# One-hot tiles of the gate matrix, laid out token by token and made by one compare-and-scale instruction per token

## The chip, the cores and the metric

The kernel runs on one core of a Trainium2 chip. The metric is device microseconds (us) of one execution, lower is better. A NeuronCore has a matrix engine (TensorE, PE in the profile; its weight loads stand apart as PEld), a vector engine (DVE), a scalar engine (ACT), GpSimd (POOL) and a queue engine that only issues transfers (SP). Each engine runs its own instruction stream in order; semaphores order the streams against each other. The operands lie in SBUF, matmul results in PSUM. [...]

## The reference, cut to what matters

Two layers, each a token mixer followed by a PEER feed-forward block with 128 x 128 = 16384 experts. The block picks 128 experts for each of 512 tokens by product keys (8 heads, 16 each) and weighs them with a softmax:

```
s, i = lax.top_k(scores, PEER_TOPK)
cand_s = s[..., 0, :, None] + s[..., 1, None, :]
top_s, sel = lax.top_k(cand_s, PEER_TOPK)
gate = jax.nn.softmax(top_s, axis=-1)
act = gelu(einsum('td,ted->te', hx, u_sel))
out = einsum('te,ted->td', gx * act, v_sel)
```

The first 128 tokens are computed by gathering rows of `peer_u` and `peer_v`. For the other 384 tokens the kernel works densely over all experts: it needs a matrix G of gates, G[i, j, token], zero but for the 128 chosen experts (i, j) of a token. That matrix is the sum over the 128 chosen of onehot(j) x onehot(i) x gate, which is a matmul of two one-hot matrices per token, contracted over the chosen experts.

## The kernel before

A layer is a mixer (L324 on) and `peer` (L826 on). In `peer` come the query projections with the first top-16 search, then a routing part in which several kinds of work are blended, then a dense part (L1122 on) that goes over 128 chunks of 128 experts.

The routing part works through a list `main` of steps with weights (WC, WP, WG, WT, WO, meant as relative lengths): `cands`, eight `pick`s and `gates` per group of 128 tokens, `spread_sel`, and for each of the 48 blocks of eight tokens a step `onehot` of weight WO. `blend` sprinkles two other lists over `main` in proportion to the weights: 68 chunks of the dense hidden layer computed ahead (`s_ahead`, L857: 24 matmuls of 384 columns each, with operands split into a high and a low part) and the gathers of the first tokens. The list is cut in three parts; the third holds all the one-hot steps. With the weights of before the parts get 10, 10 and 48 of the 68 chunks. A scheduler then sets the order of each engine's stream.

One chunk takes weights through `split_next` (L255): ACT makes the high part, and DVE or POOL, in turns, the low part (L266, tile `wsp`). `gather_load` (L867) is issued on POOL, `gather_use` (L873) runs on DVE. `pick` (L971 to L983) runs top-16 searches and compares on DVE and a product on POOL (L983). `gates` has two integer instructions with an immediate scalar on DVE (L998, L999).

A one-hot step (L1026 to L1040) handles eight tokens with tiles of 128 partitions (the chosen experts) by 128 x 8 halfwords, the eight tokens innermost. Four instructions of 1024 elements make the four tiles: `oi` (L1035, DVE: equal to the index i), `x2` (L1036, POOL: times the low part of the gate), `x1` (L1037, DVE: times the high part) and `oj` (L1038, DVE). One row `sel[n]` of eight tokens is broadcast over the 128 columns. Then `onehot_mm` (L1042) runs the block before: for each token two matmuls (L1055), `oj` as the stationary and `x1`, then `x2` as the moving operand, so 16 matmuls of 128 columns per block and 768 per layer. Neighbouring columns of one token lie eight halfwords apart. ACT moves the results out (L1057). Three sets of tiles rotate; L1037, L1038 and L1036 of a block wait for the matmuls of an earlier block in the same set.

Of the kernel before, what the change touches and what calls it, by code (L numbers as in the profile page):

```python
# [11 lines left out]
F16 = mybir.dt.float16  # L12
# [3 lines left out]
ALU = mybir.AluOpType  # L16
# [3 lines left out]
P = 128  # L20
# [8 lines left out]
NK = 128  # L29
# [12 lines left out]
APER, AOFF, ADEL = 2, 1, 4  # L42
SIDE = (0, 1, 2, 3, 13, 18, 8, 9, 10, 11, 14, 15, 16, 17)
TAILW = 0.0
WC, WP, WG, WT, WO = 3.0, 2.8, 3.0, 1.0, 1.9
GSP = 0.9
GEND = 4
PO = 1
# [11 lines left out]
TB = 8  # L60
# [49 lines left out]
def body(ctx, tc, A, tap=None):  # L110
    nc = tc.nc
    V, S, G, TE = nc.vector, nc.scalar, nc.gpsimd, nc.tensor
# [11 lines left out]
    def nm(p):  # L124
        cnt[0] += 1
        return f"{p}{cnt[0]}"
# [3 lines left out]
    def bank(shape=(P, T)):  # L130
        return psp[0].tile(list(shape), F32, tag="ps", name=nm("ps"))
# [4 lines left out]
    def s2t(name, shape=(P, T), dt=F32):  # L136
        return s2.tile(list(shape), dt, tag="s2", name=nm(name))
# [12 lines left out]
    def C(n):  # L150
        o, w = COFF[n]
        return const[:, o:o + w]
# [673 lines left out]
    def peer(l):  # L826
        with ExitStack() as pctx:
# [6 lines left out]
            sel = {n: m.tile([P, TD], F16, name=f"sel{n}") for n in ("i", "j", "g1", "g2")}  # L834
# [27 lines left out]
            pace, adas = {}, []  # L862
# [38 lines left out]
            with ExitStack() as rctx:  # L901
                rt = rctx.enter_context(tc.tile_pool(name=f"route{l}", bufs=1))
                rpool[:] = rt, 3
                SV = [s2t("SV", (P, NH, 2, TOPK)) for _ in range(NT)]
                SF = [s2t("SF", (P, NH, 2, TOPK)) for _ in range(NT)]
                iot = rt.tile([P, NK, TB], F16, name="iot")
                G.tensor_copy(iot, C("iota").unsqueeze(2).to_broadcast([P, NK, TB]))
                keys = []
                for q in range(4):
                    kq = s2t("keys", (P, 4, P))  # L910
# [113 lines left out]
                gbs, ohr, pend = {}, [], []  # L1024

                def onehot(b):  # L1026
                    if not ohr:
                        ohr.extend([[s2t("oh", (P, NK, TB), F16) for _ in range(4)] for _ in range(3)])
                    oj, oi, x1, x2 = ohr[b % 3]
                    t0 = b * TB  # L1030

                    def bc(n):
                        return sel[n][:, t0:t0 + TB].unsqueeze(1).to_broadcast([P, NK, TB])

                    V.tensor_tensor(oi, iot, bc("i"), op=ALU.is_equal)  # L1035
                    pace["G"] = G.tensor_tensor(x2, oi, bc("g2"), op=ALU.mult)  # L1036
                    V.tensor_tensor(x1, oi, bc("g1"), op=ALU.mult)  # L1037
                    pace["V"] = V.tensor_tensor(oj, iot, bc("j"), op=ALU.is_equal)  # L1038
                    onehot_mm()
                    pend.append(b)  # L1040

                def onehot_mm():  # L1042
                    if not pend:
                        return
                    b = pend.pop()
                    oj, oi, x1, x2 = ohr[b % 3]
                    t0 = b * TB
                    if t0 % GB == 0:
                        gbs[0] = rt.tile([P, NK, GB], F32, tag="gb", name=nm("gb"), bufs=2)
                    gb = gbs[0]  # L1050
                    for t4 in range(TB // 4):
                        pt = bank((P, 4, NK))
                        for tt in range(4):
                            for q, xg in enumerate((x1, x2)):
                                TE.matmul(pt[:, tt], oj[:, :, t4 * 4 + tt], xg[:, :, t4 * 4 + tt], start=(q == 0), stop=(q == 1))  # L1055
                        o = t0 % GB + t4 * 4
                        S.activation(gb[:, :, o:o + 4].rearrange("p i t -> p t i"), pt, AF.Copy, scale=1.0 / GSC)  # L1057
                    if t0 % GB == GB - TB:
                        nc.sync.dma_start(gd[t0 // GB], gb)
# [23 lines left out]
                for t in range(1, NT):  # L1083
                    oh = [(WO, lambda b=b: onehot(b)) for b in range((t - 1) * P // TB, t * P // TB)]
                    nx = steps(t + 1) if t + 1 < NT else []
                    for i in range(len(oh)):
                        main.append(oh[i])
                        if nx:
                            main.append(nx.pop(0))
                    main += nx  # L1090
# [6 lines left out]

                main.insert(-EG, (0.0, early_ge))
                main += [(0.5, onehot_mm), (TAILW, lambda: None)]
                sl = [lambda c=c: s_ahead(c) for c in range(SPILL)]  # L1100
                gs = [lambda n=n: gather_step(n) for n in range(GPRE + 2)] if GPRE else []
                cuts = [0, len(steps0), len(steps0 + steps1), len(main)]
                ws = [sum(w for w, _ in main[a:b]) for a, b in zip(cuts, cuts[1:])]
                at = [0, round(SPILL * ws[0] / sum(ws)), round(SPILL * (ws[0] + ws[1]) / sum(ws)), SPILL]
                g1 = int(GFRAC * len(gs))
# [5 lines left out]
                for i, g in enumerate(gf):  # L1111
                    n = w - (i == NG // w - 1)
# [155 lines left out]
    for l in range(L):  # L1268
        mixer(l)
        peer(l)  # L1270
# [56 lines left out]
```

## Time and profile before

| | before |
|---|---|
| median of 3 runs, us | 3853.39 (3843.79 to 3864.01) |
| profiled execution: span, us | 3864.3 |
| PE busy, us (share) | 3636.7 (94%) |
| DVE busy, us (share) | 3061.0 (79%) |
| POOL busy, us (share) | 2206.7 (57%) |
| ACT busy, us (share) | 1494.1 (39%) |
| L1055, one-hot matmuls | 1536, busy 374.7 us |
| L1036, product on POOL | 96, busy 208.4 us |
| L1035, L1037, L1038 on DVE | 96 each, busy 96.9, 106.4 and 192.9 us |

The profile gives no time of the profiled execution other than its span, which is 0.3 us above the slowest of the three timed runs and 10.9 us above their median; what lies around the span is too small to be seen here. Matmuls are pipelined: one starts before the last has ended, so the busy time of PE counts each instant once, and the distance from start to start says what one matmul costs in a stream. The same holds on DVE, where an instruction starts a little before the one ahead of it has ended.

### The profile page before, as it was taken

What the parts mean: (1) busy time and instruction counts of PE and PEld (TensorE: products, weight loads), DVE (VectorE), ACT (ScalarE), POOL (GpSimd) and SP (SyncE); (2) the same over time, 40 slices, a digit from 0 to 9 for tenths busy, and PEclk for the clock granted to TensorE, in tenths of its full rate; (3) what the DMA queues carried; (4) which work ended last, traced back from release to release, by engine and by line L of the source; (5) the groups of instructions that cost most, each with busy time, mean ns of one, the idle gap of its engine ahead of it and who ended that gap; (6) DMA issues with size and microseconds to landing.
All of it is one profiled execution on the core that took longest, in us unless ns stands there. A gap on an engine that the chain in (4) does not pass through costs nothing. (4 is left out here: it accounts for less than half of the span.)

```text
span 3864.3 us, 51554 instructions
## 1 busy us (share of the span) xinstructions
PE 3636.7 (94%) x18154; PEld 3097.8 (80%) x18154; DVE 3061.0 (79%) x5457; ACT 1494.1 (39%) x2361; POOL 2206.7 (57%) x1440
## 2 busy tenths in 40 slices
PE   5999898899999999999998999999999999999998
PEld 4787688778788888888776877887888888888887
DVE  4765489988659999999848456999886798778888
ACT  4443263344443333333353424334344433333333
POOL 3532285656446677887627204366554566767765
PEclk7886799889789999999988789998887999999999
DMA  5223253455469999999713224245554899889885
GB/s 180 77 67 103 93 186 119 159 181 179 154 227 336 340 338 322 330 331 330 265 60 93 66 77 143 90 141 177 179 170 174 308 340 336 286 303 315 308 297 214
DMA packets 349859, 810.70 MB, mean 210 GB/s; under 512 B 45216, under 2 KB 178080, under 8 KB 346272
## 3 DMA queue, kind: packets, MB, share of 16 engines
q1 hardware_dynamic: 275872, 538.94, 41.5%
q0 software_dynamic: 73728, 268.47, 19.3%
q8 instruction: 142, 2.33, 0.2%
q14 instruction: 117, 0.96, 0.1%
HBM read 722.89 MB, written 84.41 MB: 209 GB/s over the span
## 5 line engine op out<-in xcount | busy, mean ns | idle before, releaser
L283 PE MATMUL pss<-hi,wsp 128*128 128x384 f32 (+1 forms) x5168 | 1148.0, 378 | 47.5 <-DVE wsp L266 15.7
L1174 PE MATMUL ps<-vv,wg 128*128 128x512 f32 x4608 | 1098.8, 396 | 58.9 <-ACT wg L1147 29.7
L283 PEld LDWEIGHTS pss<-hi,wsp 128*128 128x128 f32 x5168 | 1021.1, 208 | 120.4 <-DVE wsp L266 17.9
L1174 PEld LDWEIGHTS ps<-vv,wg 128*128 128x128 f32 x4608 | 867.7, 190 | 257.3 <-ACT wg L1147 38.5
L266 POOL TENSOR_TENSOR wsp<-raw,wsp 128x1024 fp32r<-128x1024 f32 x185 | 479.1, 2590 | 439.6 <-ACT wsp L265 420.3
L1157 POOL TENSOR_TENSOR vv<-raw,vv 128x512 fp32r<-128x512 f32 x256 | 387.2, 1513 | 369.5 <-ACT vv L1156 347.0
L265 ACT ACTIVATE wsp<-raw 128x1024 fp32r<-128x1024 f32 x341 | 359.8, 1057 | 587.4 <-PE pss L283 397.6
L283 PE MATMUL pss<-lo,wsp 128*128 128x384 f32 (+1 forms) x2584 | 534.9, 348 | 0.0
L283 PEld LDWEIGHTS pss<-lo,wsp 128*128 128x128 f32 x2584 | 463.7, 189 | 21.9 <-issue 0.5
L873 DVE SCALAR_TENSOR_TENSOR row<-row,hx 128x1024 f32<-128x1024 f32 x256 | 426.3, 1670 | 33.0 <-DMA row<-u,ex 32.8
L881 DVE SCALAR_TENSOR_TENSOR ox<-row,wx,ox 128x1024 f32<-128x1024 f32 x254 | 420.0, 1654 | 15.4 <-DMA row<-v,ex 11.7
L1156 ACT ACTIVATE vv<-raw 128x512 fp32r<-128x512 f32 x512 | 293.7, 621 | 255.2 <-DMA raw<-v 227.4
L1055 PE MATMUL ps<-oh,oh 128*128 128x128 f16 x1536 | 374.7, 414 | 5.5 <-DVE oh L1038 5.5
L867 POOL DMA_INDIRECT row<-v,ex x256 | 339.4, 1326 | 66.3 <-issue 47.7
L1147 ACT ACTIVATE wg<-ge 128x384 fp32r<-128x384 f32 x256 | 132.3, 522 | 617.6 <-DVE ge L1145 506.7
L867 POOL DMA_INDIRECT row<-u,ex x256 | 338.0, 1320 | 50.2 <-issue 32.5
L1036 POOL TENSOR_TENSOR oh<-oh,selg 128x1024 f16<-128x1024 f16 x96 | 208.4, 2173 | 266.2 <-PE ps L1055 252.8
L1055 PEld LDWEIGHTS <-oh 128*128 128x128 f16 x1536 | 217.1, 146 | 136.8 <-issue 9.7
L1157 DVE TENSOR_TENSOR vv<-raw,vv 128x512 fp32r<-128x512 f32 x256 | 254.1, 993 | 61.1 <-ACT vv L1156 61.0
L1145 DVE TENSOR_TENSOR ge<-ge,g 128x192 f32<-128x192 f32 x496 | 245.6, 532 | 28.1 <-DMA g<-gscr 18.3
L1057 ACT ACTIVATE gb<-ps 128x512 f32<-128x512 f32 x192 | 213.2, 1111 | 122.7 <-PE ps L1055 120.5
L266 DVE TENSOR_TENSOR wsp<-raw,wsp 128x1024 fp32r<-128x1024 f32 x156 | 219.9, 1410 | 38.0 <-ACT wsp L265 37.1
(459 smaller groups left out, 4102.8 us busy)
## 6 DMA issues: line engine op xcount, KB each, us to landing
raw<-uT SPq DMA_DIRECT2D x256, 512.0 KB
raw<-v SPq DMA_DIRECT2D x256, 512.0 KB
gscr<-gb SPq DMA_DIRECT2D x24, 2048.0 KB
g<-gscr SPq DMA_DIRECT2D x124, 384.0 KB
gespill<-ge SPq DMA_DIRECT2D x136, 192.0 KB
ge<-gespill SPq DMA_DIRECT2D x136, 192.0 KB
ada<-ada SPq DMA_DIRECT2D x96, 256.0 KB
raw<-ada SPq DMA_DIRECT2D x48, 512.0 KB
```

The lines of the kernel that those rows point to most:

```text
L265: S.activation(w[:, 0], raw, AF.Copy)
L266: (G if on_pool(i) else V).tensor_tensor(w[:, 1], raw, w[:, 0].bitcast(F32), op=ALU.subtract)
L283: TE.matmul(pt, w[:, a, k * P:(k + 1) * P], hs[k][b], start=start and n == 0, stop=stop and n == len(steps) - 1)
L867: G.indirect_dma_start(out=rows[n], out_offset=None, in_=A["u" if n < P else "v"], in_offset=bass.IndirectOffsetOnAxis(ap=ex[:, n % P:n % ...
L873: V.scalar_tensor_tensor(row, row, 1.0, hx, op0=ALU.mult, op1=ALU.mult, accum_out=dots[:, e:e + 1])
L881: V.scalar_tensor_tensor(ox, row, wx[:, e:e + 1], ox, op0=ALU.mult, op1=ALU.add)
L1055: TE.matmul(pt[:, tt], oj[:, :, t4 * 4 + tt], xg[:, :, t4 * 4 + tt], start=(q == 0), stop=(q == 1))
L1057: S.activation(gb[:, :, o:o + 4].rearrange("p i t -> p t i"), pt, AF.Copy, scale=1.0 / GSC)
L1145: V.tensor_tensor(gq, gq, g[:, :, c % IG], op=ALU.mult)
L1156: S.activation(vv[0][q], raw[:, q * T:(q + 1) * T], AF.Copy)
L1157: vlo[q] = (V, G)[q].tensor_tensor(vv[1][q], raw[:, q * T:(q + 1) * T], vv[0][q].bitcast(F32), op=ALU.subtract)
L1174: end[0] = TE.matmul(acc[t][d2], wg[a][:, ts_], vv[b][d2], start=(c == 0 and a == 0 and b == 0), stop=(c == NK - 1 and a == 1))
```

## The change

Each one-hot tile now has the token as its outer index: 8 x 128 halfwords, the 128 columns of a token side by side. Each token's 128 columns of each tile are made by one DVE instruction that takes the index row `iot` (now 128 columns, no longer repeated eight times), compares it with one number per partition read from SBUF and, for `x1` and `x2`, multiplies by a second such number. So a block has 24 DVE instructions of 128 elements in place of three of 1024 on DVE and one of 1024 on POOL. The tile `oi` is gone. The two matmuls per token read adjacent columns. The weight WO of a one-hot step in the blend goes from 1.9 to 2.6, by which the three parts get 9, 8 and 51 chunks.

```diff
-WC, WP, WG, WT, WO = 3.0, 2.8, 3.0, 1.0, 1.9
+WC, WP, WG, WT, WO = 3.0, 2.8, 3.0, 1.0, 2.6
...
-                iot = rt.tile([P, NK, TB], F16, name="iot")
-                G.tensor_copy(iot, C("iota").unsqueeze(2).to_broadcast([P, NK, TB]))
+                iot = rt.tile([P, NK], F16, name="iot")
+                V.tensor_copy(iot, C("iota"))
...
-                        ohr.extend([[s2t("oh", (P, NK, TB), F16) for _ in range(4)] for _ in range(3)])
-                    oj, oi, x1, x2 = ohr[b % 3]
...
-                    V.tensor_tensor(oi, iot, bc("i"), op=ALU.is_equal)
-                    pace["G"] = G.tensor_tensor(x2, oi, bc("g2"), op=ALU.mult)
-                    V.tensor_tensor(x1, oi, bc("g1"), op=ALU.mult)
-                    pace["V"] = V.tensor_tensor(oj, iot, bc("j"), op=ALU.is_equal)
+                        ohr.extend([[s2t("oh", (P, TB, NK), F16) for _ in range(3)] for _ in range(3)])
+                    oj, x1, x2 = ohr[b % 3]
+                    for k in range(TB):
+                        at = lambda n: sel[n][:, b * TB + k:b * TB + k + 1]
+                        V.tensor_scalar(oj[:, k], iot, at("j"), None, op0=ALU.is_equal)
+                        V.tensor_scalar(x1[:, k], iot, at("i"), at("g1"), op0=ALU.is_equal, op1=ALU.mult)
+                        pace["V"] = V.tensor_scalar(x2[:, k], iot, at("i"), at("g2"), op0=ALU.is_equal, op1=ALU.mult)
...
-                                TE.matmul(pt[:, tt], oj[:, :, t4 * 4 + tt], xg[:, :, t4 * 4 + tt], start=(q == 0), stop=(q == 1))
+                                TE.matmul(pt[:, tt], oj[:, t4 * 4 + tt], xg[:, t4 * 4 + tt], start=(q == 0), stop=(q == 1))
```

In the changed file the three new instructions are L1032 (`oj`), L1033 (`x1`) and L1034 (`x2`), and the matmuls are L1051.

DVE before, early in the one-hot part of the first layer (`oh` are the one-hot tiles, `selg` the gates, `row` a gathered row, `wsp` a chunk's low part):

```order
L1038 TENSOR_TENSOR oh_5642<-iot,selj 128x1024
L1035 TENSOR_TENSOR oh_5639<-iot,seli 128x1024
L1035 TENSOR_TENSOR oh_5643<-iot,seli 128x1024
L1037 TENSOR_TENSOR oh_5636<-oh_5635,selg_3285 128x1024
L1038 TENSOR_TENSOR oh_5634<-iot,selj 128x1024
L873 SCALAR_TENSOR_TENSOR row_6778,dots<-row_6778,hx 128x1024
L266 TENSOR_TENSOR wsp_6887<-raw_6885,wsp_6887 128x1024
```

and DVE now, in the same part, with the steps of a `pick` (L915 to L981) between:

```order
L1033 TENSOR_SCALAR oh_5542<-iot,seli,selg_3285 128x128
L1034 TENSOR_SCALAR oh_5543<-iot,seli,selg_3286 128x128
L918 MATCH_REPLACE tw_5795<-r_5570,cv_5568 128x50
L971 TENSOR_REDUCE r_5570<-eq_5710 128x8
L971 TENSOR_REDUCE r_5570<-eq_5713 128x8
L916 MAX_INDEX r_5570<-r_5570,cv_5568 128x8 x5
L1033 TENSOR_SCALAR oh_5542<-iot,seli,selg_3285 128x128
L1032 TENSOR_SCALAR oh_5541<-iot,selj 128x128
```

Before, whole tiles stood between other work; now the short instructions of a block and the steps of a `pick` are interleaved one by one.

PE now, late in the one-hot part (L283 are a chunk's matmuls); before, the 16 of a block (here L1051) stood together and the 24 matmuls of a chunk stood together:

```order
L283 MATMUL pss_8796<-hi_3241,wsp_8590 128x384 x2
L283 MATMUL pss_8796<-hi_3246,wsp_8590 128x384
L1051 LDWEIGHTS oh_5535
L1051 MATMUL ps_8771<-oh_5536,oh_5535 128x128
L283 MATMUL pss_8796<-hi_3246,wsp_8590 128x384
L283 MATMUL pss_8796<-hi_3251,wsp_8590 128x384 x2
L1051 LDWEIGHTS oh_5535
L1051 MATMUL ps_8771<-oh_5537,oh_5535 128x128
```

In the last stretch single one-hot matmuls now stand inside a chunk, each behind the DVE instruction that makes its operand.

## Rows read from the trace of the kernel before

**Rows 1.** Windows: length, busy PE, PEld, DVE, ACT, POOL (instructions), granted clock, DMA share, GB/s.
```profile
692.00:1121.00 429.00, 417.72 (x1916) 346.50 (x1916) 343.75 (x502) 179.56 (x198) 244.89 (x128) 0.85 0.50 170
2400.00:2577.00 177.00, 159.98 (x843) 146.03 (x843) 172.10 (x791) 62.08 (x88) 83.76 (x61) 0.97 0.37 110
2577.00:3005.00 428.00, 423.07 (x1928) 352.94 (x1929) 347.21 (x501) 180.98 (x200) 242.62 (x129) 0.83 0.50 171
```

**Rows 2.** The same windows, instructions on the one-hot tiles alone (PE, PEld, DVE, POOL).
```profile
692.00:1121.00 429.00, 187.53 (x768) 108.39 (x768) 187.22 (x144) 104.86 (x48) 0.85 0.50 170
2577.00:3005.00 428.00, 187.21 (x768) 108.70 (x768) 199.31 (x144) 103.51 (x48) 0.83 0.50 171
```

**Rows 3.** Waits in 692 to 1121: who for whom, us in total, times, longest.
```profile
DVE oh L1037 <- PE ps L1055: 71.9, 27, 5.4
```

**Rows 4.** Timeline of PE: start, length, line and tiles, count [idle before].
```profile
534.57 1.05 PE L935 MATMUL ps<-keys,qT 128*128 128x128 f32 x8
...
723.70 11.43 PE L1055 MATMUL ps<-oh,oh 128*128 128x128 f16 x48 [5.48 <-DVE oh L1038]
736.58 5.49 PE L283 MATMUL pss<-hi,wsp 128*128 128x384 f32 x16 [1.45 <-ACT ge L854]
...
884.15 3.93 PE L1055 MATMUL ps<-oh,oh 128*128 128x128 f16 x16
887.72 3.17 PE L283 MATMUL pss<-hi,wsp 128*128 128x384 f32 x16
890.72 1.55 PE L283 MATMUL pss<-lo,wsp 128*128 128x384 f32 x8
```

**Rows 5.** PE in three short windows: us, busy (count), granted clock, DMA.
```profile
724.00:734.00 10.00, 10.00 (x44) 0.50 0.18 54
884.20:887.70 3.50, 3.50 (x17) 1.00 0.22 71
737.00:741.50 4.50, 4.50 (x15) 0.50 1.08 451
```

**Rows 6.** Timeline of DVE where nothing holds it, from four places.
```profile
371.53 0.48 DVE L196 TENSOR_SCALAR acc<-raw,silu_c 128x512 f32<-128x512 f32 x1
...
686.79 0.23 DVE L998 TENSOR_SCALAR EI<-EI 128x128 int32<-128x128 int32 x1
686.94 0.22 DVE L999 TENSOR_SCALAR EI<-EI 128x128 int32<-128x128 int32 x1
687.07 0.28 DVE L993 TENSOR_TENSOR r<-r,mx 128x128 f32<-128x128 f32 x1
...
738.92 0.68 DVE L1035 TENSOR_TENSOR oh<-iot,seli 128x1024 f16<-128x1024 f16 x1
739.52 0.68 DVE L1037 TENSOR_TENSOR oh<-oh,selg 128x1024 f16<-128x1024 f16 x1
...
1538.47 1.21 DVE L873 SCALAR_TENSOR_TENSOR row<-row,hx 128x1024 f32<-128x1024 f32 x1
```

**Rows 7.** Group of gathered rows in 692 to 1121: count, busy us, mean ns, idle.
```profile
L873 DVE SCALAR_TENSOR_TENSOR row<-row,hx 128x1024 f32<-128x1024 f32 x24 | 46.1, 1922 | 2.8 <-DMA row<-u,ex 2.8
```

**Rows 8.** Timeline of DVE and POOL about one long instruction of DVE.
```profile
794.65 0.94 POOL L867 DMA_INDIRECT row<-u,ex  x1 [0.30 <-issue]
...
794.94 0.23 DVE L998 TENSOR_SCALAR EI<-EI 128x128 int32<-128x128 int32 x1
795.09 6.70 DVE L999 TENSOR_SCALAR EI<-EI 128x128 int32<-128x128 int32 x1
795.61 1.91 POOL L1036 TENSOR_TENSOR oh<-oh,selg 128x1024 f16<-128x1024 f16 x1
797.46 2.39 POOL L266 TENSOR_TENSOR wsp<-raw,wsp 128x1024 fp32r<-128x1024 f32 x1
799.79 1.89 POOL L1036 TENSOR_TENSOR oh<-oh,selg 128x1024 f16<-128x1024 f16 x1
```

More of the change, by code (lines that the diff above doesn't have):

```diff
@@ L1027, in onehot @@
                     if not ohr:
-                        ohr.extend([[s2t("oh", (P, NK, TB), F16) for _ in range(4)] for _ in range(3)])
-                    oj, oi, x1, x2 = ohr[b % 3]
-                    t0 = b * TB
-                    def bc(n):
-                        return sel[n][:, t0:t0 + TB].unsqueeze(1).to_broadcast([P, NK, TB])
-                    V.tensor_tensor(oi, iot, bc("i"), op=ALU.is_equal)
-                    pace["G"] = G.tensor_tensor(x2, oi, bc("g2"), op=ALU.mult)
-                    V.tensor_tensor(x1, oi, bc("g1"), op=ALU.mult)
-                    pace["V"] = V.tensor_tensor(oj, iot, bc("j"), op=ALU.is_equal)
+                        ohr.extend([[s2t("oh", (P, TB, NK), F16) for _ in range(3)] for _ in range(3)])
[5 more added lines that the diff above has]
+                        pace["V"] = V.tensor_scalar(x2[:, k], iot, at("i"), at("g2"), op0=ALU.is_equal, op1=ALU.mult)
                     onehot_mm()
@@ L1045, in onehot_mm @@
                     b = pend.pop()
-                    oj, oi, x1, x2 = ohr[b % 3]
+                    oj, x1, x2 = ohr[b % 3]
                     t0 = b * TB
```

## The prediction

> **What bounds the kernel now.** I went from the matmuls of the one-hot tiles to the stretches in which they run. All the one-hot work lies in two stretches of 429 and 428 us, one per layer, 22% of the span of 3864.3 us [rows 1]. There PE is busy 417.7 and 423.1 us, DVE 343.8 and 347.2, POOL 244.9 and 242.6. The reader should see that PE has next to no idle time, and that the long wait of DVE is for PE: 71.9 us in the first stretch until the matmuls of an earlier block have set a tile free [rows 3]. So PE sets the end of both stretches.
>
> What fills PE there comes from starts in its timeline. 48 one-hot matmuls in a row take 11.43 us, and less the 0.41 us of the last one (it ends as a single matmul does) that is 0.234 us from start to start; in another place 16 take 3.93, which gives 0.235 [rows 4]. [...] Adjacent columns do better: 8 matmuls of 128 columns in f32 take 1.05 us with the tail of the last, at most 0.131 each [rows 4]. A chunk's matmuls do follow the clock: 16 take 3.00 us at the upper level (887.72 to 890.72) and 5.28 at the lower (736.58 to 741.86) [rows 4, 5]. A chunk of 24 is then 4.4 us or 7.9 us.
>
> Sum for one stretch: 768 x 0.235 = 180 us of one-hot matmuls, 48 chunks x 4.4 = 211, together 391; the 30 us or so that are left go to chunks at the lower level, since the granted clock of the stretches is 0.85 and 0.83 [rows 1].
>
> **The change part by part.**
>
> *Matmuls.* 768 x 0.235 = 180 us become at most 768 x 0.131 = 101 per stretch. Three more chunks come in by the new weight: 51 x 4.4 = 224. PE would need 325 us at the upper level, some 100 less than now. That is no gain by itself; DVE is next in line.
>
> *POOL.* The product goes, 104.9 and 103.5 us [rows 2]; 140 us of POOL stay in each stretch (244.9 - 104.9). The copy that repeated the index row leaves POOL for a DVE copy of 128 columns, twice in the program: nothing.
>
> *DVE, what goes.* 144 instructions per stretch, 187.2 and 199.3 us, mean 193 [rows 2]. The rest of DVE's work is 345.5 - 193 = 152 us.
>
> *DVE, what comes.* 48 blocks x 24 = 1152 instructions of 128 elements. No row has this one, so I build it. Where nothing holds them, L1035 with 1024 elements starts 0.60 us ahead of the next, and L998 and L999 with 128 elements take 0.28 for two, 0.14 each [rows 6]. That is (0.60 - 0.14)/896 = 0.00051 us per element, and 0.074 us that doesn't depend on the length. A scalar read from memory costs more than an immediate: by the lengths 0.23 (128 elements) and 0.68 (1024), 512 elements should last 0.42, and L196, with such a scalar, lasts 0.48 [rows 6]; 0.06 us for it. L1035 handles halfwords at two per 0.001 us, and L873, f32, takes 1.21 us for the same 1024 [rows 6], so halfwords doubled the rate there; L196 in f32 already has the rate of L1035. For the new instruction I take double again, 128 x 0.00026 = 0.033. Sum: 0.033 + 0.074 + 0.06 = 0.167 us, and 1152 x 0.167 = 192 us. Bounds: 0.107 if the scalar read hides behind the instruction ahead (123 us); 0.167 + 0.06 for two thirds of them, if the second scalar of L1033 and L1034 costs as much again (238 us); 0.20 at the rate that the rows show (230 us); 0.265 at half of it (305 us).
>
> [...]
>
> *DVE held by POOL.* L999 lasts 0.22 us as a rule and 6.70 us at 795.09: it ends only after three POOL instructions of 1.91, 2.39 and 1.89 us that stand back to back [rows 6, 8]. So an instruction of this kind waits out POOL's whole instruction, and several. How much do such waits take now? One-hot: 193 less 144 x 0.64 (between 0.60 and 0.68) = 92 leaves 101 us. Gathered rows: 24 x (1.92 - 1.21) = 17 [rows 6, 7]. L999: 6.5. Together 125 of POOL's 245 us, 51%. Of the 24 us outside the one-hot tiles, 10 fall to L1036 by its share of POOL's time (105/245), so the rest of DVE falls to 142 us with 14 us of waits in it. For the 140 us of POOL that stay I take the same 51%, 71 us, of which 57 are new on the one-hot instructions. Bounds: nothing, and all of it, 126.
>
> [...]
>
> *Sum.* 142 + 192 + 57 = 391 us of DVE. A stretch in which DVE is the bound has it busy 172.1 of 177 us, 0.972 [rows 1], so 402 us. The chunks moved in add 2.6 us (1.5 low parts on DVE and the waits for 1.5 on POOL); the search part that they leave gains too little to count. 405 against 428.5: 23.5 us less, twice, 47 us. From 3864.3 that is 3817; the span lies 10.9 us above the median of the runs, so 3806, rounded to **3805 us**. The stretches would then end with DVE, no longer with PE, and PE's 100 us would mostly turn into waits for one-hot tiles.
>
> **The rivals.**
>
> *POOL shuts DVE out nearly all the time (slower).* Short instructions offer POOL a way in after each 0.17 us, and DVE will have one of them next almost always. For: the 6.70 us. Against: DVE lost only 51% so far, and L998 beside L867 lasts its usual 0.23 [rows 8]. At 80% of 140 us the new waits are 98: (142 + 192 + 98)/0.972 + 2.6 = 447, 18.5 more per stretch, 3890 us; at 100%, 3948. It decides from (428.5 - 2.6) x 0.972 - 334 = 80 us on, that is 67% of POOL's time.
>
> *The second scalar costs like the first (slower).* 46 us more: 437/0.972 + 2.6 = 452, 3900 us. No row has two such scalars, for or against. Break-even is at a mean of 0.187 us per instruction, other terms as above.
>
> *The instructions are cheap (much faster).* With the scalar read hidden, 123 us: (142 + 123 + 57)/0.972 + 2.6 = 334, 94.5 less per stretch, 3664 us, just above PE's 325. For: L998's 0.14 shows that the fixed part is small, and reads are small too. Against: L196's 0.06. [...]
>
> [...]
>
> [...]
>
> **How the numbers follow.** Forecast 0.40 (its own range 3750 to 3860), cheap instructions 0.24, POOL 0.13, second scalar 0.11, no fast mode 0.06, clock 0.06. Half a per cent, 19 us, is what a measurement of this kernel tells from no change. Faster than 3834: three quarters of the forecast, 0.30, the cheap case, 0.24, and 0.01 of others: 0.55. Within: 0.09 of the forecast and 0.06 of the four slow cases: 0.15. Slower: 0.30. The range goes from 3650 (the cheap case a little below its sum) to 3925, past the second scalar and POOL at 90%; outside lie the single rate, POOL in full, half of the clock case and a tail of the cheap one, about 0.2.
>
> **What would show it.** L1051 from start to start at 0.13 us or less at both clocks (else the first step is wrong). L1032 about 0.17 us apart, L1033 and L1034 the same (0.11: cheap; 0.23: second scalar). Some of them 1 to 3 us long, each ending with a POOL instruction, 57 us in sum per stretch. DVE busy over 0.95 of the stretches, PE with some 80 us idle there behind L1032 to L1034, and L1037's wait for PE gone. If the stretches last under 350 us, or DVE idles in them, the sum on DVE was wrong; if they last over 430, a wait or price above was too low.

## The result and the profile after

The changed kernel takes 3889.47 us, median of 12 runs (3872.42 to 3900.33), against 3857.10 (3843.79 to 3880.70, also 12): a ratio of 1.0075, 95% interval 1.0052 to 1.0097. It is slower by 0.75%, where 3805 us and a gain were forecast.

The table cuts the span into phases, here and in all later runs by the same marks: a stretch goes from the start of its first one-hot instruction on DVE to the start of its last one-hot matmul; a dense part from the start of the first to that of the last `back` matmul (L1174 before, L1170 after). All in us, of the profiled executions.

| | stretch 1 | stretch 2 | dense 1 | dense 2 | span |
|---|---|---|---|---|---|
| before | 428.0 | 427.7 | 804.4 | 840.7 | 3864.3 |
| after | 420.1 | 423.5 | 811.9 | 865.9 | 3881.6 |
| difference | -7.9 | -4.2 | +7.5 | +25.2 | +17.3 |

So the stretches gain 12 us where 47 were forecast, and the dense parts, on which the forecast had no term, lose 33; -3 is left for everything else. Single runs lie up to some 20 us from their median: the profiled execution of before lies 7 us above its median, that of after 8 below, so the spans differ by 17 and the medians by 32, and the table does not place the 15 between them.

Windows of the two stretches after, same columns as [rows 1]:
```profile
691.70:1112.00 420.30, 345.87 (x2023) 291.50 (x2023) 415.97 (x1502) 173.19 (x206) 136.31 (x80) 0.85 0.52 175
2576.70:3000.50 423.80, 337.74 (x2006) 287.46 (x2004) 418.35 (x1502) 172.16 (x204) 139.57 (x81) 0.85 0.50 175
```
and of the instructions on one-hot tiles alone, PE, PEld and DVE, beside [rows 2]:
```profile
691.70:1112.00 420.30, 108.94 (x768) 56.58 (x768) 293.12 (x1152) 0.85 0.52 175
2576.70:3000.50 423.80, 106.24 (x768) 56.49 (x768) 296.26 (x1152) 0.85 0.50 175
```
DVE has taken PE's place: busy 415.97 of 420.3, 99%. PE has 74 idle and POOL half its old work. The one-hot tiles cost DVE 293 us a stretch; the forecast had 192 + 57 = 249.

Waits in the first stretch after, columns as in [rows 3]. DVE's wait for PE, 71.9 us there, is 1.8 us now, and PE waits for DVE:
```profile
PEld L1051 <- DVE oh L1032: 35.0, 97, 3.5
...
PE ps L1051 <- DVE oh L1033: 31.6, 60, 7.4
```

The price of the new instructions is read from starts where nothing holds them. Timeline of DVE after, which answers [rows 6]:
```profile
763.10 0.24 DVE L1032 TENSOR_SCALAR oh<-iot,selj 128x128 f16<-128x128 f16 x1
763.26 0.30 DVE L1033 TENSOR_SCALAR oh<-iot,seli,selg 128x128 f16<-128x128 f16 x1
763.48 0.30 DVE L1034 TENSOR_SCALAR oh<-iot,seli,selg 128x128 f16<-128x128 f16 x1
763.70 0.24 DVE L1032 TENSOR_SCALAR oh<-iot,selj 128x128 f16<-128x128 f16 x1
...
889.46 0.30 DVE L1033 TENSOR_SCALAR oh<-iot,seli,selg 128x128 f16<-128x128 f16 x1
889.68 2.44 DVE L1034 TENSOR_SCALAR oh<-iot,seli,selg 128x128 f16<-128x128 f16 x1
892.05 0.24 DVE L1032 TENSOR_SCALAR oh<-iot,selj 128x128 f16<-128x128 f16 x1
```
L1032, with one scalar from memory, takes 0.16 us to the next start; L1033 and L1034, with two, take 0.22 each. Over longer runs of starts the figures are 0.162 and 0.223. The L1034 of 2.44 us is taken as one held by POOL, which starts this at the same moment and ends it within 0.04 us of L1034's end (timeline of POOL after):
```profile
889.68 2.40 POOL L266 TENSOR_TENSOR wsp<-raw,wsp 128x1024 fp32r<-128x1024 f32 x1 [4.57 <-issue]
```

Timeline of PE after, one-hot matmuls in a row, beside [rows 4]:
```profile
833.47 1.07 PE L1051 MATMUL ps<-oh,oh 128*128 128x128 f16 x16
...
994.38 1.96 PE L1051 MATMUL ps<-oh,oh 128*128 128x128 f16 x32
```
Less the 0.22 us of the last, 15 distances take 0.85 and 31 take 1.74: 0.056 us each at a granted clock of 1.00, where it was 0.235.

### The profile page after: what moved, and what is told of

The parts are those of the page before. It is cut to its first block, busy times and chain, and to the rows that moved or that the text cites. A ratio compares the mean times of both kernels' runs of the same rounds, so it can differ in the third digit from the quotient of the medians.

```text
span 3881.6 us, 53386 instructions
## 1 busy us (share of the span) xinstructions
PE 3459.4 (89%) x18154; PEld 2945.7 (76%) x18154; DVE 3209.4 (83%) x7475; ACT 1466.2 (38%) x2361; POOL 1978.9 (51%) x1342
## 5 line engine op out<-in xcount | busy, mean ns | idle before, releaser
L283 PE MATMUL pss<-hi,wsp 128*128 128x384 f32 (+1 forms) x5168 | 1132.2, 372 | 100.1 <-DVE wsp L266 46.0
L1170 PE MATMUL ps<-vv,wg 128*128 128x512 f32 x4608 | 1108.5, 397 | 85.0 <-ACT wg L1143 48.5
L283 PEld LDWEIGHTS pss<-hi,wsp 128*128 128x128 f32 x5168 | 989.6, 203 | 177.1 <-DVE wsp L266 50.9
L1170 PEld LDWEIGHTS ps<-vv,wg 128*128 128x128 f32 x4608 | 868.6, 191 | 295.0 <-ACT wg L1143 63.3
L266 POOL TENSOR_TENSOR wsp<-raw,wsp 128x1024 fp32r<-128x1024 f32 x185 | 467.5, 2527 | 613.2 <-ACT wsp L265 537.6
L283 PE MATMUL pss<-lo,wsp 128*128 128x384 f32 (+1 forms) x2584 | 547.0, 351 | 0.0
L283 PEld LDWEIGHTS pss<-lo,wsp 128*128 128x128 f32 x2584 | 464.2, 190 | 21.6 <-issue 0.5
L873 DVE SCALAR_TENSOR_TENSOR row<-row,hx 128x1024 f32<-128x1024 f32 x256 | 414.9, 1631 | 31.2 <-DMA row<-u,ex 31.0
L881 DVE SCALAR_TENSOR_TENSOR ox<-row,wx,ox 128x1024 f32<-128x1024 f32 x254 | 419.4, 1651 | 25.2 <-DMA row<-v,ex 21.3
L983 POOL TENSOR_TENSOR eq<-eq,cid 128x400 f32<-128x400 f32 x128 | 163.7, 1297 | 299.1 <-DVE eq L981 299.1
L1051 PE MATMUL ps<-oh,oh 128*128 128x128 f16 x1536 | 215.2, 234 | 100.3 <-DVE oh L1033 65.1
L1141 DVE TENSOR_TENSOR ge<-ge,g 128x192 f32<-128x192 f32 x496 | 232.8, 504 | 45.5 <-DMA ge<-gespill 37.0
L1033 DVE TENSOR_SCALAR oh<-iot,seli,selg 128x128 f16<-128x128 f16 x768 | 263.5, 344 | 5.1 <-PE ps L1051 5.1
L1034 DVE TENSOR_SCALAR oh<-iot,seli,selg 128x128 f16<-128x128 f16 x768 | 267.0, 349 | 0.1
```

Source lines behind the costliest of these rows:

```text
L266: (G if on_pool(i) else V).tensor_tensor(w[:, 1], raw, w[:, 0].bitcast(F32), op=ALU.subtract)
L283: TE.matmul(pt, w[:, a, k * P:(k + 1) * P], hs[k][b], start=start and n == 0, stop=stop and n == len(steps) - 1)
L873: V.scalar_tensor_tensor(row, row, 1.0, hx, op0=ALU.mult, op1=ALU.mult, accum_out=dots[:, e:e + 1])
L881: V.scalar_tensor_tensor(ox, row, wx[:, e:e + 1], ox, op0=ALU.mult, op1=ALU.add)
L1033: V.tensor_scalar(x1[:, k], iot, at("i"), at("g1"), op0=ALU.is_equal, op1=ALU.mult)
L1034: pace["V"] = V.tensor_scalar(x2[:, k], iot, at("i"), at("g2"), op0=ALU.is_equal, op1=ALU.mult)
```

## The experiments

Two accounts stood after the result. In one, the second scalar of L1033 and L1034 costs about as much as the first was put at, and the rest of the loss comes from work behind the stretches. In the other, DVE is held by POOL (or by the number of instructions as such), and the later phases are noise. The letters in the expectations below are each run's own. Every ratio is to before, timed together with that kernel.

**One scalar in place of two** (`e1_one_scalar`; the gates are left out of G, all else stays):
```diff
-V.tensor_scalar(x1[:, k], iot, at("i"), at("g1"), ...)
+V.tensor_scalar(x1[:, k], iot, at("i"), 1.0, ...)       # x2 likewise
```


> The changed kernel, but L1033 and L1034 multiply by an immediate 1.0 in place of the gate read from SBUF (the gates are left out of G). Theory A (the second scalar is the mis-sized term): each of the 768 instructions per stretch falls from 0.223 to 0.162 us from start to start, DVE's sum in a one-hot stretch falls by 47 us, the stretches end some 40 to 47 us earlier each (375 to 382 us in place of 420 and 423), and the kernel takes about 3800 us. Rival B (the loss lies in the dense part, whose transfers now stand in another order): the stretches shorten in the same way, but the dense parts stay at about 812 and 866 us (804 and 841 before). Rival C (the stretches are held by something else than DVE's sum): the stretches shorten by less than 15 us.

Measured: 3790.84 us, ratio 0.9818 (0.9781 to 0.9855). Stretches 375.7 and 380.1, so 44 us less each, by one operand. Timeline of DVE in this run:
```profile
756.97 0.24 DVE L1033 TENSOR_SCALAR oh<-iot,seli 128x128 f16<-128x128 f16 x1
757.13 0.24 DVE L1034 TENSOR_SCALAR oh<-iot,seli 128x128 f16<-128x128 f16 x1
757.29 0.24 DVE L1032 TENSOR_SCALAR oh<-iot,selj 128x128 f16<-128x128 f16 x1
```
All three forms stand 0.16 apart, so 768 x 0.061 = 47 us are the second scalar's. The count of instructions stayed (same columns as the one-hot windows above):
```profile
694.50:1070.20 375.70, 91.25 (x768) 52.01 (x768) 260.10 (x1152) 0.88 0.57 196
```
DVE's one-hot time fell by 33 us here and by 40 in layer two, less than 47, as the time beyond the starts rose from 60 to 73 (1152 x 0.162 = 187 of the 260.1). The dense parts are still long, 828.1 and 859.7; this profiled execution is the slowest of five, 17 us above their median.

**The old weight of a one-hot step** (`e2_wo19`): is the weight, which moves chunks, at fault?
```diff
-WC, WP, WG, WT, WO = 3.0, 2.8, 3.0, 1.0, 2.6
+WC, WP, WG, WT, WO = 3.0, 2.8, 3.0, 1.0, 1.9
```


> The changed kernel with the blend weight WO back at 1.9, so 10, 10 and 48 chunks. Theory A (DVE sets the stretch, the weight moves little): the stretches are 1 to 5 us shorter, the search parts as much longer, total within 10 us of 3889. Rival B (the order of the transfers behind the stretch makes the dense part slow, and the weight takes part in setting it): the dense parts go back towards 804 and 841 us and the total to 3860 to 3870.

Measured: 3875.8 us, ratio 1.0043 (1.0017 to 1.0068). Stretches 418.9 and 424.3, as in after; dense parts 825.3 and 850.0. The weight doesn't bring before's dense parts back: their sum is 1675.3 us, after's 1677.8. The split between the layers differs, but a second execution of after moves it as well (`e8_after_again` below), so that shift is not shown to be the weight's. Neither expectation is met cleanly, and the interval overlaps that of after.

**Adjacent reads alone** (`e3_adjacent_reads`): before, with the matmuls reading its tiles as if they lay token by token, so that G is made of the wrong elements and only the step of the reads changes.
```diff
-TE.matmul(pt[:, tt], oj[:, :, t4 * 4 + tt], xg[:, :, t4 * 4 + tt], ...)
+TE.matmul(pt[:, tt], adj(oj)[:, t4 * 4 + tt], adj(xg)[:, t4 * 4 + tt], ...)
```


> The kernel before, but the matmuls read its tiles as if each token's 128 columns lay side by side (G gets wrong entries; the tiles are made as before). This is the change's gain on PE alone. Theory A: matmuls 0.056 us apart in place of 0.235, PE loses 137 us per stretch, DVE with its 345 us and POOL's product become the bound, the stretches last 350 to 370 us and the kernel about 3740. Rival (the stretch waits in circles between PE, DVE and POOL): the stretches stay above 400 us, and the kernel above 3820.

Measured: 3720.75 us, ratio 0.9635 (0.9597 to 0.9674); stretches 352.3 and 355.5, matmuls 0.056 apart. The reads alone are worth 76 and 72 us a stretch, and DVE (344.5 us busy in the first) is the bound behind them. The new layout pays; the way in which after fills the tiles gives it back. DVE's dense order here is before's, instruction for instruction, and the dense parts are 812.9 and 842.5.

**Two tokens innermost** (`e4_pairs`): a version meant to keep both, the 1024-element instructions and cheap reads. A tile is 4 pairs of tokens by 128 columns by 2 tokens, so a matmul reads every second halfword.
```diff
+TI = 2
-... s2t("oh", (P, NK, TB), F16)
+... s2t("oh", (P, TB // TI, NK, TI), F16)
-TE.matmul(pt[:, tt], oj[:, :, t4 * 4 + tt], ...)
+a, c = divmod(t4 * 4 + tt, TI)
+TE.matmul(pt[:, tt], oj[:, a, :, c], ...)
```


> The kernel before with two tokens innermost in place of eight: the four tile instructions of a block stay (1024 elements, broadcasts), and neighbouring columns of a token lie two halfwords apart. If a step of two halfwords costs the matmul nothing, they come 0.056 us apart, and if DVE keeps its rate with runs of two halfwords (0.60 us per instruction), the stretches last 350 to 370 us and the kernel about 3740. Rival 1: the matmul takes 0.1 us or more at this step: stretches 370 to 400. Rival 2: DVE falls to half its rate on runs of two (1.1 us): its sum grows by 72 us per stretch and the kernel is not faster than before.

Measured: 3715.59 us (3712.95 to 3716.34), ratio 0.9627 (0.9591 to 0.9663); stretches 354.1 and 357.5, dense 802.0 and 839.8. Operations on the one-hot tiles in this run (count, then shortest, median and longest duration in ns, first to last start):
```profile
L1058 PE MATMUL ps<-oh,oh x1536: 217/218/308, 698.4 to 2856.1; 128*128 128x128 f16 x192
L1037 DVE TENSOR_TENSOR oh<-iot,seli x96: 665/679/2910, 691.0 to 2847.4; 128x1024 f16<-128x1024 f16 x96
```
and two rows of PE's timeline, the first at a granted clock of 1.00, the second at 0.50:
```profile
1017.95 1.10 PE L1058 MATMUL ps<-oh,oh 128*128 128x128 f16 x16
...
1006.21 1.89 PE L1058 MATMUL ps<-oh,oh 128*128 128x128 f16 x16 [2.62 <-DVE oh L1040]
```
Their granted clock, third column from the end in these windows:
```profile
1006.30:1008.00 1.70, 1.70 (x17) 1.70 (x18) 1.70 (x1) 0.72 (x1) 1.70 (x1) 0.50 0.00 0
1017.90:1019.00 1.10, 1.10 (x18) 0.93 (x16) 1.10 (x2) 0.85 (x1) 0.19 (x1) 1.00 1.09 432
```
The last of the 16 lasts 0.22 us in the first row and 0.31 in the second; from start to start it is 0.058 and 0.105 us on average. In after, with adjacent reads, the starts stand 0.056 apart at 1.00 and 0.107 at 0.50 (between 730 and 733 us): here every second halfword costs as little as adjacent ones and the matmuls follow the clock, and DVE keeps its 0.68 us for 1024 elements.

**Another order of the work behind the stretches.** The program's instructions are ordered by a simulated timeline (L1322 of before), so a change in one part also rewrites the order of the others. Layer two's dense part has 886 DVE instructions from its first to its last `back` matmul. Comparing two runs line by line (lines out plus lines in), after differs from before in 310, e3 and e4 from before in none. The weight TAILW, of a step that does nothing, shifts a chunk or two in the routing part and so changes that order without touching a one-hot instruction: 70 lines from after's, 316 from before's. `e5_pairs_order` is e4 with it, `e6_before_order` is before with it.
```diff
-TAILW = 0.0
+TAILW = 5.0
```


> The kernel with two tokens innermost (e4) with a blend weight of 5.0 for the empty last step (TAILW), which shifts one or two chunks within the routing part and by that lets the scheduler write the dense part in nearly the order of the changed kernel (on DVE 4 of the last 600 rows differ from it, 206 from the kernel before). Theory A (that order is what makes the dense parts long): the two dense parts last 1672 to 1690 us together in place of 1642, and the kernel takes 3740 to 3765 us in place of 3716. Rival B (the dense parts are long for another reason that goes with the per-token instructions, or vary from run to run): 1640 to 1656 us, and 3710 to 3725 us.

> The kernel before with TAILW at 5.0, so its one-hot tiles are as before and its dense part stands in nearly the order of the changed kernel. Theory A: dense parts 1672 to 1690 us together in place of 1645, the kernel 25 to 45 us above 3855. Rival B: dense parts 1640 to 1656, the kernel within 10 us of 3855.

Measured: e5 3756.38 us, ratio 0.9746 (0.9711 to 0.9781), against e4's 3715.59; e6 3912.19, ratio 1.0154 (1.0125 to 1.0182). Start ranges of the dense matmuls in layer two, first before, then after, then e6:
```profile
L1174 PE MATMUL ps<-vv,wg x2304: 387/389/796, 3012.4 to 3853.1; 128*128 128x512 f32 x192
```
```profile
L1170 PE MATMUL ps<-vv,wg x2304: 387/389/796, 3004.3 to 3870.2; 128*128 128x512 f32 x192
```
```profile
L1174 PE MATMUL ps<-vv,wg x2304: 387/390/632, 3037.5 to 3898.0; 128*128 128x512 f32 x192
```
840.7, 865.9 and 860.5 us: with the same instructions in another order, layer two's dense part takes 20 us more, in e5 as well (862.5 against 839.8). Layer one's, whose order under TAILW is nearer to before's (230 lines in e6, against 405 from after's), stays: 803.5 in e6, 805.1 in e5. The two parts together, 1667.6 us in e5 and 1664.0 in e6, fall 4 and 8 us short of the range expected. The rest of e5's and e6's loss is outside the dense parts: between stretch and dense part e5 has 16.8 and 15.4 us against e4's 10.3 and 6.4, e6 18.4 and 13.3 against before's 11.6 and 8.0 (matmuls of one to two more chunks stand there, which is what TAILW moved), and e6 loses 9.5 us more ahead of layer two's stretch. After itself loses nothing there (6.6 and 4.0). e6's whole loss is larger than expected.

Where layer two's time goes shows when its dense part is cut at the start of the 69th chunk's `back` matmuls (all in us):

| | before | e3 | e4 | e7 | after | e8 | e5 | e6 |
|---|---|---|---|---|---|---|---|---|
| first 68 chunks | 295.4 | 298.1 | 298.2 | 297.7 | 316.2 | 311.7 | 320.6 | 311.2 |
| other 60 | 545.3 | 544.4 | 541.6 | 541.5 | 549.7 | 545.0 | 542.0 | 549.3 |

So 16 to 21 us of after's loss lie in the first 68. (e7 and e8 follow below. e7's order on DVE differs from before's in 200 lines and costs nothing here, so not every other order does.) DVE's waits in that part (who for whom, us in total, times, longest), before, then after, then e6:
```profile
DVE ge L1145 <- DMA ge<-gespill: 7.4, 10, 1.6
```
```profile
DVE ge L1141 <- DMA ge<-gespill: 37.0, 22, 5.0
```
```profile
DVE ge L1145 <- DMA ge<-gespill: 47.2, 37, 4.1
```
These chunks read back the hidden layer that the stretches stored (`ge`, four buffers in turn). In SP's order before, two such loads stand side by side nine times (in e4 nine, in e7 seven); after, where it is twice, and in e5 and e6, once each, they mostly alternate with loads of `v` (tile `raw`). A passage of each:
```
before                        after
ge <- gespill                 ge <- gespill
ge <- gespill                 raw <- v
raw <- v                      ge <- gespill
g <- gscr (two)               g <- gscr (two)
ge <- gespill                 raw <- v
raw <- v                      ge <- gespill
```
Waits of SP, the queue that issues them, in the same stretch, before and then after:
```profile
SPq L1137 <- DVE wg L1148: 63.7, 39, 4.7
```
```profile
SPq L1133 <- DVE wg L1144: 95.1, 44, 7.2
```
The queue stands before a `ge` load until the `wg` instruction of DVE has read the buffer's last content.

**After once more** (`e8_after_again`, one execution): is the dense part's loss repeatable?

> The changed kernel once more, for a second profile. If the dense parts' length belongs to the program, they last 1670 to 1685 us together again (1678 the first time); if it varies from run to run, they may be near 1645.

Measured: 3887.43 us; stretches 420.6 and 424.6, dense 820.6 and 856.7, sum 1677.3 against 1677.8. The sum repeats; its split between the layers moves by 9 us.

**Six buffers for the loads in dispute** (`e9_after_ge6` is after with them, `e10_order_ge6` is e5 with them):
```diff
-ge = ger[c % 4]
-if c > 3:
+ge = ger[c % NGE]        # NGE = 6
+if c >= NGE:
```


> The changed kernel with six buffers in place of four for the tile ge, which brings the hidden chunks back from memory in the dense part; its order in the dense part stays near the changed kernel's. Theory A (in that order the loads of ge are issued too late, DVE waits 37 us for them in layer two's first 68 chunks): that wait falls below 10 us, the dense part of layer two lasts 838 to 848 us in place of 850 to 866, and the kernel takes 3860 to 3878 us. Rival (the late loads are only a symptom, the transfers as a whole are the bound): the wait moves to the loads of v or of the gathered rows and the dense parts last as long as before the edit, 3880 to 3890 us.

> The kernel of e5 (two tokens innermost, dense part in the changed kernel's order) with six buffers for ge. Theory A: the wait of DVE for ge (57.6 us in e5) falls below 10, layer two's dense part goes from 862 to 840 to 848 us, the kernel from 3756 to 3735 to 3742. Rival: no change, 3750 to 3760.

Measured: e9 3860.5 us, ratio 1.0006 (0.9989 to 1.0024); dense 813.3 and 846.6, the wait for `ge` 21.6 us where under 10 were expected. e10 3735.87, ratio 0.9676 (0.9654 to 0.9698), dense 2 849.4, wait 33.3. With two more buffers layer two's dense part is 10 to 19 us shorter, its first 68 chunks take 303.6 and 303.7 us, and in after all of the median's loss is gone (of the 26 us between the profiled spans 18 lie in the dense parts); the wait shrinks but doesn't vanish. So late `ge` loads go with the order's cost, as a part of it and not all that was claimed. The buffers are not isolated, for they rewrite the order too: on DVE 112 lines of layer two's dense part differ between after and e9, 94 between e5 and e10.

**The product off POOL** (`e7_pairs_dve`): e4, with the tile `x2` made on DVE.
```diff
-pace["G"] = G.tensor_tensor(x2, oi, bc("g2"), op=ALU.mult)
+V.tensor_tensor(x2, oi, bc("g2"), op=ALU.mult)
```


> The kernel with two tokens innermost (e4) with the product that POOL made moved to DVE. Theory A (DVE waits out POOL's instructions, so POOL's product costs DVE more than doing it itself): DVE gains 48 x 0.60 = 29 us of work per stretch and loses some 80 us of waits, its sum falls from 348 to about 300 us, the stretches last 305 to 325 us and the kernel about 3640 to 3670. Rival (the waits for POOL are hidden elsewhere): DVE's sum rises by 29 us, the stretches last 380 us and the kernel about 3770.

Measured: 3628.48 us (3620.63 to 3634.51), ratio 0.9411 (0.9381 to 0.9442); stretches 306.1 and 304.3. Windows of the first stretch, e4 and then this run:
```profile
691.00:1045.10 354.10, 276.56 (x1914) 263.90 (x1914) 345.19 (x494) 166.17 (x197) 247.65 (x128) 0.90 0.57 199
```
```profile
695.60:1001.70 306.10, 264.04 (x1915) 254.74 (x1914) 290.62 (x540) 165.81 (x197) 140.16 (x79) 0.94 0.66 228
```
Timeline of DVE in this run, where nothing holds it:
```profile
849.76 0.68 DVE L1039 TENSOR_TENSOR oh<-oh,selg 128x1024 f16<-128x1024 f16 x1
850.37 0.68 DVE L1038 TENSOR_TENSOR oh<-oh,selg 128x1024 f16<-128x1024 f16 x1
850.97 0.68 DVE L1040 TENSOR_TENSOR oh<-iot,selj 128x1024 f16<-128x1024 f16 x1
```
DVE takes 48 instructions of these more (494 to 540 in all, a little other work having moved) and is busy 55 us less. At 0.60 us the 48 add 29, so by this sum some 84 us of waiting on DVE went with the 108 us of POOL's work that went; that the waiting was for POOL is inferred from this.

**The fastest** (`e11_pairs_dve_ge6`): e7 with the six buffers.

> The fastest kernel so far (e7: two tokens innermost, all four tile instructions on DVE) with six buffers for ge. Theory A: its dense parts waited little for ge (839 us in layer two), so within 10 us of 3628. Rival (more room helps every order): 10 to 20 us faster.

Measured: 3612.25 us (3610.76 to 3628.81), ratio 0.9370 (0.9343 to 0.9398); dense 801.5 and 829.3, against e7's 809.2 and 839.2. The best of all, 277 us below the changed kernel. It is 16 us faster than e7, so the rival expectation held and not the first. Only 3 of these are in the first 68 chunks of layer two (294.9 against 297.7 us), where DVE waited for `ge` no more than 6.8 us in e7; the others lie where no `ge` is loaded or in layer one, and go with the new order that the buffers bring (230 lines).

## Why the prediction was wrong

*Right: the matmuls.* They were put at 0.131 us or less and came, where nothing holds them, to 0.056 at a granted clock of 1.00 and 0.107 at 0.50; before, they stood 0.235 and 0.234 apart at these two. e3 changes nothing but the reads and has the 0.056 too. Also right: the bound moves from PE to DVE, PE waits for L1032 to L1034, and DVE's wait for PE goes.

*Right: the price with one scalar.* 0.167 forecast, 0.162 measured for L1032, below the 0.20 that stands in the bounds for the rate of the rows. The three terms behind 0.167 (fixed part, elements, scalar) were not measured one by one: the 0.033 for the elements, at double the rows' rate, is the author's estimate, and no run shows it by itself. None of the three new forms comes below 0.16.

*Wrong: "L1033 and L1034 the same".* The step that prices the new instructions at 0.167 each counted nothing for the second scalar. It costs 0.061 us, what the first was put at: 384 x (0.162 + 0.223 + 0.223) = 233.5 us in place of 192. That is the second rival, held at 0.11, whose break-even of 0.187 us per instruction the mean of 0.203 passes. e1 takes it away and 44 us of a stretch go. This is the term of the sum on DVE that was too small.

*About right: POOL.* 293.1 - 233.5 = 60 us beyond the starts on one-hot instructions, 57 forecast as waits for POOL; in e1 the same difference is 73 and 69. So POOL does not shut DVE out (first rival): 60 is 44% of its 136 us.

*Too high: the rest of DVE.* 142 forecast, 416.0 - 293.1 = 123 measured, 34 less than before's 343.8 - 187.2 = 157 in that stretch, where the forecast took off 10. Gathered rows wait less now; their group in the first stretch after, beside [rows 7]:
```profile
L873 DVE SCALAR_TENSOR_TENSOR row<-row,hx 128x1024 f32<-128x1024 f32 x23 | 32.0, 1393 | 1.8 <-DMA row<-u,ex 1.8
```
46.1 - 32.0 = 14 us of the 34; the casts of L977 in the picks (11.2 to 4.9 us) and L999 (6.9 to 0.4) give 6 each. That the short instructions took waits over from long ones would fit this, but is not shown. And DVE is busy 99% of the stretch, not 97%. So the second rival's 452 became 420: -8 where the forecast had -23.5 and the rival +23.5. The sum on DVE is 416 against 391; 41.5 of price and 3 of waits on one side, 19 of rest on the other. That the stretches still gained 8 and 4 us is so in part luck: one error made up for half of the other.

*Missing: the dense parts.* The sum ran as if nothing behind the stretches changed, a term put at nothing without a reason. They cost 33 us, half of the 65 by which the span missed the 3817 of the sum (35 are the stretches', -3 the rest's). Without them the span would have fallen by 15 us, so the sign was lost here, and most of the forecast gain at the second scalar. That another order alone costs 20 us of layer two is shown by e5 and e6, and that e3 and e4, with before's order, lose none there agrees. That late `ge` loads carry part of it fits the waits (36 to 58 us in after, e8, e5 and e6 against 7.4 before), the place (the first 68 chunks) and e9 and e10, but their buffers change the order too, so it is not isolated. Layer one's loss (7.5, 16 and 8.9 us in after, e8 and e9; 24 and 21 in e1 and e2) goes with an order that differs too, but no run isolates it, and e3 lost 8.5 there under before's order: it stays open. Which rows of the order do it is open as well.

*The other rivals.* Cheap instructions (0.107) and no faster rate than the rows' (0.20) both fell with 0.162. The clock was granted at 0.85 in both stretches, hardly other than the 0.85 and 0.83 before, though the slow matmuls had gone and PE idled for 74 us in the first, where it had 11 before; PE still was not the bound, and no run shows what lowers its clock.

## What to carry to other kernels

Count the operands that an instruction reads from memory per partition, each of them (the second cost 0.061 us here): when one long instruction becomes many short ones, what each takes comes that many times (here eight at 0.203 us on average, 1.62, in place of one at 0.60). When the reader of a tile is slow, try an inner step just small enough for the reader (here two instead of eight took a matmul from 0.235 us to 0.058; four was not run) and keep the long instructions for the writer (0.60 us per 1024 elements with eight as with two). And where a scheduler orders the whole program, put a term for the phases that weren't touched into the range, and compare phase by phase before explaining the total.

## What the runs showed of the hardware

- A matmul of 128 columns whose operands step by 8 halfwords took 0.235 us from start to start at a granted clock of 1.00 and 0.234 at 0.50 (before, [rows 4, 5]); by 2 halfwords 0.058 and 0.105 (e4), adjacent 0.056 and 0.107 (after). The stationary and the moving operand changed together, so no run tells which of them sets the price.
- A 16-bit `tensor_scalar` of 128 elements took 0.162 us from start to start with one scalar read from memory and 0.223 with two (after): 0.061 us for the second, and in e1, without it, all three forms stand 0.16 apart. No run takes the first away.
- A 16-bit `tensor_tensor` with broadcasts in runs of only two halfwords kept 0.60 us from start to start per 1024 elements (e7; duration 0.68 in e4 and e7), as in before, in runs of eight [rows 6].
- More work on DVE made DVE less busy: 345 to 291 us when POOL's product moved onto it (e4 and e7), while the stretch became 48 us shorter; by the sum above, an estimate, some 84 us of waits went for 29 of work.
